# Spreading the small products of a triangular inverse over four tiles of TensorE, and moving one product into their first visit

## The chip, the cores and the metric

The kernel runs on one core of a Trainium2 chip. The metric is the device time of one execution in microseconds (us); lower is better. Before the change it is 2568.02 us, the median of three runs (2565.74 to 2568.44).

## What is computed

One layer of a streaming encoder, for 1024 new frames and 32 frames of a running stream. Every frame goes through a normalisation, one large combined projection, and then two groups of heads: differential attention, and an RWKV-7 recurrence whose state is a 64x64 matrix per head. The two results are gated, joined and projected back, and the input is added. Cut to what matters here:

```python
xn = rms_norm(x, norm_g)
proj = xn @ w_in                      # q, k, v, g_att, p_rw, g_rw
o  = diff_attention(q, keys, vals, q_pos, k_pos, lam)
...
def step(S, inp):                     # one token of the recurrence
    r_t, w_t, k_t, v_t, a_t, b_t = inp
    sa = jnp.einsum('bhij,bhj->bhi', S, a_t)
    S = S * w_t[:, :, None, :] + sa[..., None] * b_t[:, :, None, :] + v_t[..., None] * k_t[:, :, None, :]
    y = jnp.einsum('bhij,bhj->bhi', S, r_t)
    return S, y
...
out = jnp.concatenate([att_out, rw_out], axis=-1) @ w_out
return x + out, k, v, s_final, p_rw[:, -1:]
```

## The kernel before, in words

**Projections.** The tokens are worked on in two halves, A (544 columns, in pieces of 288 and 256) and B (512 columns). `proj` (L102 is the line of the matmul helper `mm` that it calls) multiplies one 128-column block of weights by all tokens: 16 steps of k, three products each (a high and a low part of weights and of tokens), into a PSUM tile `pj`. The weights come as raw pieces `wr` by DMAs issued on GpSimd's queue (POOL, L241), ScalarE rounds them to `wh` (ACT, L234), VectorE forms the rest `wl` (DVE, L235).

**Streams.** All other work is cut into generators (`chs`, `dns`, `qks`, `ats` and so on) that are called between the matmuls of a projection. `clk` is a running estimate of TensorE's time that `mm` adds to (with a divisor `ways`) and `shaped` adds 95 ns to whenever the tile shape of a product changes; a generator yields a delay from the table `LAT`, and its next part is issued at the first call at which `clk` has passed that delay. The chain stream `chs` is called after every step of k, the others after two or four. TensorE executes everything in the order in which it was issued, so that a product that comes before its operand is ready holds all the projections behind it.

**The recurrence.** It is done by chunks of 64 tokens. For each pair of heads (u, 16 in all with both halves) there are two sub-blocks of four chunks, except that in half A the second has five: 32 sub-blocks, 24 with cn = 4 and 8 with cn = 5, each with ng = 2 cn blocks (a chunk and one of two heads). A token's update inside a chunk needs the inverse of a unit triangular 64x64 matrix. Its two 32x32 diagonal blocks are inverted on VectorE (the loop of L799 and L801 in `rw_down`), go to DRAM (`dt`) and come back; the block that joins them is the product of three 32x32 matrices.

**The chain of a sub-block, `rw_chain`.** It first transposes V into the upper 64 rows of `UV` (L844 and L845 read it out of PSUM), loads the inverses into `TT` (the matrix that is put together) and into `t01` (a tile with tag k2, which the trace calls `k`), and has VectorE transpose a part of them (L861). Then come three visits to TensorE, with a yield between each two, in which other work is issued. All three write the one PSUM tile `ch`:

1. ng products 32x32, of the strict block of `MM` with `u0`, into rows 32 to 63 of `ch`; ScalarE reads them out as `wt` (L866), into rows 32 to 63 of `UV`.
2. after `t10`, ng products 32x32, of `wt` with `t01`, into rows 0 to 31; ScalarE reads them into `TT` in two pieces (L873).
3. after `x0`, ng products 64x64, of the strict part of `MM` with V; ScalarE reads them back into `MM` in two pieces (L880).

A product of float32 stands in the trace as two weight loads and two matmuls, so that a visit of ng = 8 has 16 matmuls and one of ng = 10 has 20. Every product of the first visit uses the same 32x32 tile of the array, as does every one of the second; those of the third lie in rows 64 to 127 of the array and go by turns to columns 0 to 63 and 64 to 127. After the three visits the chain walks over its chunks one by one (three products each, delays `c0` to `c3`); L931 is VectorE's last read of `ch` for a chunk.

Of the kernel before, what the change touches and what calls it, by code (L numbers as in the profile page):

```python
# [46 lines left out]
def build(tc, I, O):  # L47
    nc = tc.nc
    V, S, G, PE = nc.vector, nc.scalar, nc.gpsimd, nc.tensor
# [6 lines left out]
    def T(shape, tag, dt=F32, bufs=1):  # L56
        cnt[0] += 1
        return sb.tile(shape, dt, tag=tag, name=f"{tag}_{cnt[0]}", bufs=bufs)

    def PT(tag, bufs, shape=(128, 512)):  # L60
        cnt[0] += 1
        return ps.tile(list(shape), F32, tag=tag, name=f"{tag}_{cnt[0]}", bufs=bufs)
# [6 lines left out]
    def bank(tag, shape=(128, 512)):  # L69
        if tag not in held:  # L70
            held[tag] = PT(tag, 1, shape)
        return held[tag]
# [14 lines left out]
    def shaped(k, m):  # L87
        now = tuple(next(z for z in (32, 64, 128) if x <= z) for x in (k, m))
        if now != mode[0]:
            clk[0] += 95.0  # L90
            mode[0] = now

    def mm(out, lhsT, rhs, start=True, stop=True, ways=1):
        n, m = 1, 1
        for d in rhs.shape[1:]:
            n *= d
        for d in lhsT.shape[1:]:
            m *= d
        shaped(lhsT.shape[0], m)
        load = 0.83 * m + 5.0  # L100
        clk[0] += (max(0.4375 * n + 6.0, load) if rhs.dtype == F32R else 2 * max(0.84 * n, load)) / ways
        PE.matmul(out, lhsT, rhs, start=start, stop=stop)  # L102

    def tr(out, in_, idn):
        shaped(*in_.shape)
        clk[0] += 110.0
        PE.transpose(out, in_, idn)  # L107
# [73 lines left out]
    def dma(out, in_):  # L181
        if out.dtype == F32R:
            out, in_ = out.bitcast(F32), in_.bitcast(F32)
        nc.sync.dma_start(out, in_)
# [83 lines left out]
    for k, tag in enumerate(RAW):  # L268
# [7 lines left out]
        a, eng = (acc[1], G) if pool else (acc[0], V)  # L276
# [141 lines left out]
    def lat(key, half):  # L418
        return LAT[key + "AB"[half]]
# [262 lines left out]
    def flat(t):  # L682
        return t.rearrange("p c t -> p (c t)")
# [43 lines left out]
    def after(sub, stream, kind, back):  # L727
        j = sub - back
        return lambda: j < 0 or (kind, j // 2, j % 2) in stream.done
# [98 lines left out]
    def rw_chain(half, i, sub, st):  # L828
        lo, hi = SUBS[half][sub]
        cn = hi - lo  # L830
        ng = 2 * cn
        gsub = 2 * (8 * half + i) + sub
        AR, MM, MMg, dt, t_m = (st[sub][n] for n in ("AR", "MM", "MMg", "dt", "t_m"))
        PL, v = st["PL"], st["v"]
        UV = T([128, cn, 2, 64], "UV")
        UVf = UV.rearrange("p c h t -> p c (h t)")
        yield lat("bk0", half)
        p = bank("ch")
        for j in range(2):
            tr(p[:, 128 * j:128 * j + 128], flat(v)[:, 64 * lo + 128 * j:64 * lo + 128 * j + 128], ident)  # L840
        if cn == 5:
            tr(p[0:64, 256:384], v[:, 8, :], ident)
        pv = p[:, 0:256].rearrange("p (a b) -> p a b", b=128)
        S.copy(UVf[64:128, 0:4:2, :], pv[0:64])  # L844
        S.copy(UVf[64:128, 1:4:2, :], pv[64:128])  # L845
        if cn == 5:
            S.copy(UVf[64:128, 4, :], p[0:64, 256:384])
        if sub == 1:
            chs.done.add(("vread", 8 * half + i))
        TT = TTb[:, 0:cn]  # L850
        dtg = dt.rearrange("b (c h) s t -> b h s c t", h=2)
        for b in range(2):
            for h in range(2):
                o = 64 * h + 32 * b
                dma(TT[o:o + 32, :, o:o + 32], dtg[b, h, 0:32])
        t01 = T([64, ng, 32], "k2")
        for b in range(2):
            dma(t01[32 * b:32 * b + 32], dt[b, :, 0:32, :].rearrange("g s t -> s g t"))
        UVg = UVf.rearrange("p c t -> p (c t)")[0:64, 0:32 * ng].rearrange("p (g t) -> p g t", t=32)
        u0, wt = UVg[0:32], UVg[32:64]  # L860
        V.transpose(u0.rearrange("p g t -> p (g t)"), t01[0:32].rearrange("p g t -> p (g t)"))  # L861
        yield max(1500, t_m + lat("tt", half) - clk[0])
        p = bank("ch")
        for g in range(ng):
            mm(p[32:64, 32 * g:32 * g + 32], MMg[0:32, g, 32:64], u0[:, g, :])
        S.copy(wt, p[32:64, :32 * ng].rearrange("p (a b) -> p a b", b=32))  # L866
        yield lat("t10", half)
        p = bank("ch")
        for g in range(ng):
            mm(p[0:32, 32 * g:32 * g + 32], wt[:, g, :], t01[32:64, g, :])  # L870
        pg = p[0:32, :32 * ng].rearrange("p (c h b) -> p c h b", h=2, b=32)
        for h in range(2):
            S.copy(TT[64 * h:64 * h + 32, :, 64 * h + 32:64 * h + 64], pg[:, :, h, :])  # L873
        yield lat("x0", half)
        p = bank("ch")
        for c in range(cn):
            for h in range(2):
                mm(p[64 * h:64 * h + 64, 64 * c:64 * c + 64], MM[64:128, c, h, 0:64], UV[64:128, c, h, :])
        for h in range(2):
            S.copy(MM[0:64, :, h, 0:64], p[64 * h:64 * h + 64, :64 * cn].rearrange("p (c v) -> p c v", v=64))  # L880

        yield after(gsub, pos, "post", 1)
        Y = T([128, 3, 128], "Yt")
        if sub == 0:
            Sw = T([128, 2, 64], "Sw")
            G.memset(Sw, 0.0)
            if half == 1:
                for h in range(2):
                    dma(Sw[64 * h:64 * h + 64, h, :], Spast[i, 64 * h:64 * h + 64, :])
            st["Sw"] = Sw  # L890
        order = [4, 0, 1, 2, 3] if cn == 5 else [0, 1, 2, 3]
        key = "c0"
        for c in order:
            gc = lo + c
            if c == 4:
                S_ = T([128, 2, 64], "S0")
                G.memset(S_, 0.0)
                for h in range(2):
                    dma(S_[64 * h:64 * h + 64, h, :], I["S0"][i, 64 * h:64 * h + 64, :])
            else:  # L900
                S_ = st["Sw"]
            Sf = S_.rearrange("p h t -> p (h t)")
            yield lat(key, half)
            key = "c1"
            ch = bank("ch")
            mm(ch[:, 0:128], AR[:, c].rearrange("p a t -> p (a t)"), Sf)
            RS = T([128, 128], "RS")
            S.copy(RS[high], ch[high, 0:128])  # L908
            xs = T([128, 64], "xs")
            for h in range(2):  # L910
                V.tensor_tensor(xs[64 * h:64 * h + 64], ch[low, 64 * h:64 * h + 64], MM[low, c, h, 0:64], op=ALU.add)  # L911
            SP = T([64, 2, 64], "SP")
            for h, hr in enumerate((low, high)):
                S.activation(SP[:, h, :], S_[hr, h, :], AF.Copy, scale=PL[hr, 0, gc:gc + 1])  # L914
            yield lat("c2", half)
            mm(ch[:, 128:192], TT[:, c, :], xs)
            S.copy(UV[low, c, 0, :], ch[low, 128:192])
            V.tensor_copy(UV[low, c, 1, :], ch[high, 128:192])  # L918
            yield lat("c3", half)
            for h in range(2):  # L920
                mm(ch[:, 192 + 64 * h:256 + 64 * h], MM[:, c, h, 64:192], UV[:, c, h, :])
            for h, hr in enumerate((low, high)):
                V.scalar_tensor_tensor(S_[hr, h, :], ch[low, 192 + 64 * h:256 + 64 * h], PL[low, h, gc:gc + 1],  # L923
                                       SP[:, h, :], ALU.mult, ALU.add)
            if c == 4:
                V.tensor_tensor(Y[0:64, 2, :], ch[high, 192:320], RS[high], op=ALU.add)
                G.memset(Y[64:128, 2, :], 0.0)
                for h in range(2):
                    dma(O["wkvs"][i, 64 * h:64 * h + 64, :], S_[64 * h:64 * h + 64, h, :])
            else:  # L930
                V.tensor_tensor(Y[64 * (c % 2):64 * (c % 2) + 64, c // 2, :], ch[high, 192:320], RS[high],  # L931
                                op=ALU.add)
                if gc == 7:
                    for h in range(2):
                        dma((Spast, O["wkvp"])[half][i, 64 * h:64 * h + 64, :], S_[64 * h:64 * h + 64, h, :])
        st[sub]["Y"] = Y
# [64 lines left out]
    for u in range(16):  # L1001
        half, i = divmod(u, 8)
        n, ncnk, chunks = (NA, NB)[half], (9, 8)[half], CHUNKS[half]
# [171 lines left out]
```

## Time and profile before

| what | before |
|---|---|
| median of three runs | 2568.02 us |
| lowest, highest | 2565.74, 2568.44 us |
| the profiled execution | 2568.85 us |
| its span, first to last instruction | 2567.1 us |
| mean granted TensorE clock | 0.993 of full speed |
| instructions | 48812 |
| TensorE matmul busy | 2482.5 us (97%) |
| VectorE, ScalarE, GpSimd busy | 1884.4 (73%), 1366.2 (53%), 414.1 us (16%) |

The span is what the rows of the trace add up to; 1.75 us of the profiled execution lie around it. In rows of the trace PE is TensorE's matmuls, PEld its weight loads, DVE VectorE, ACT ScalarE, POOL GpSimd and SP the queue that issues most DMAs. A matmul's duration counts from its first column to the end of a modelled pipeline, so that matmuls overlap: what one costs is the step from its start to the next one's start.

### The profile page before, as it was taken

The numbers are of one execution on the slowest core, as the hardware profiler recorded it, in microseconds if no ns is written. First come the engines' busy times: TensorE is split into PE (matmuls) and PEld (weight loads), VectorE is DVE, ScalarE is ACT, GpSimd is POOL, SyncE is SP. The second block draws the span as 40 slices with busy tenths as digits, with TensorE's granted clock in tenths as the row PEclk, the third lists the DMA queues.
The fourth block names the chain that finished last, engine by engine and source line by source line (L and its number), as shares of the span: only waits on it lengthen the run. The fifth ranks groups of instructions, "written<-read, shape, count | busy, mean of one in ns | idle before, by whom it ended". The sixth has DMA issues, their size and how long they took to land.

```text
span 2567.1 us, 48812 instructions
## 1 busy us (share of the span) xinstructions
PE 2482.5 (97%) x17128; PEld 2189.9 (85%) x17128; DVE 1884.4 (73%) x5704; ACT 1366.2 (53%) x3210; POOL 414.1 (16%) x949
## 2 busy tenths in 40 slices
PE   7999999999999999999999999999999999999999
PEld 7999999899998899977777777877777778999887
DVE  6577777777777787788788888887878888653432
ACT  6455555555556555565555555656565556232321
POOL 3211111111111111111111111111111111111000
PEclk8999999999999999999999999999999999999999
DMA  5333333333344424343333333333333345545443
GB/s 163 111 103 107 101 97 96 103 93 108 90 118 133 121 75 123 104 141 98 96 102 93 105 94 105 94 105 94 105 91 104 89 128 149 148 139 151 144 140 106
DMA packets 198662, 286.71 MB, mean 112 GB/s; under 512 B 102096, under 2 KB 115920, under 8 KB 198416
## 3 DMA queue, kind: packets, MB, share of 16 engines
q0 software_dynamic: 51088, 169.12, 22.2%
q1 hardware_dynamic: 147328, 114.47, 15.8%
q8 instruction: 135, 2.21, 0.4%
q14 instruction: 111, 0.91, 0.1%
HBM read 228.11 MB, written 37.51 MB: 103 GB/s over the span
## 4 chain that ended last, share of the span: by engine, by line
PE 64%; DVE 20%; DMA 5%; ACT 5%; issue 4%; SPq 1%; POOL 0%; DVEq 0%; ACTq 0%; POOLq 0%
PE pj L102 48%; PE ch L102 6%; DVE wl L235 4%; PE am L102 3%; DVE ts L801 3%; DVE tm L799 3%; PE sc L102 2%; PE Y L102 2%; ACT wh L234 1%; DVE Sw L923 1%; PE sc L107 1%; PE am L107 1%; DVE ca L715 1%; DMA E<-x_prompt 1%; DMA wr<-w_in 1%
## 5 line engine op out<-in xcount | busy, mean ns | idle before, releaser
L102 PE MATMUL pj<-xh,wh 128*128 128x256 f32 (+2 forms) x3888 | 1314.4, 338 | 11.8 <-ACT xh L258 6.7
L102 PE MATMUL pj<-xl,wh 128*128 128x256 f32 (+2 forms) x3888 | 1267.1, 326 | 4.1 <-DVE xl L259 4.0
L102 PE MATMUL pj<-xh,wl 128*128 128x256 f32 (+2 forms) x3888 | 1265.9, 326 | 1.1 <-DVE wl L235 1.1
L102 PEld LDWEIGHTS pj<-xh,wh 128*128 128x128 f32 x3888 | 738.4, 190 | 64.7 <-ACT xh L258 6.7
L102 PEld LDWEIGHTS pj<-xh,wl 128*128 128x128 f32 x3888 | 738.1, 190 | 55.5 <-DVE wl L235 2.6
L102 PEld LDWEIGHTS pj<-xl,wh 128*128 128x128 f32 x3888 | 739.4, 190 | 47.7 <-DVE xl L259 6.1
L234 ACT CAST wh<-wr 128x512 fp32r<-128x512 f32 x584 | 360.6, 618 | 412.8 <-PE pj L102 361.8
L235 DVE TENSOR_TENSOR wl<-wr,wh 128x512 fp32r<-128x512 f32 x584 | 401.1, 687 | 175.8 <-ACT wh L234 168.2
L241 POOL DMA_DIRECT2D wr<-w_in x517 | 277.8, 537 | 1549.2 <-DVE wl L235 653.0
L801 DVE TENSOR_TENSOR ts<-tm,ts 64x54 f32<-64x54 f32 (+35 forms) x992 | 197.9, 200 | 15.7
L799 DVE TENSOR_TENSOR tm<-ts,ms 64x54 f32<-64x54 f32 (+35 forms) x992 | 197.8, 199 | 14.9
L102 PEld LDWEIGHTS ch<-UV,MM 64*64 64x64 f32 (+2 forms) x1632 | 112.6, 145 | 41.4 <-DVE UV L918 15.5
L914 ACT ACTIVATE SP<-Sw,PL 64x64 f32<-64x64 f32 x256 | 88.4, 345 | 103.4 <-DVE Sw L923 86.0
L102 PE MATMUL ch<-UV,MM 64*64 64x64 f32 (+2 forms) x1632 | 126.2, 230 | 8.3 <-DVE UV L918 5.4
L235 DVE TENSOR_TENSOR wl<-MM,wh 128x512 fp32r<-128x512 f32 x64 | 44.0, 689 | 89.2 <-ACT wh L234 89.2
L234 ACT CAST wh<-MM 128x512 fp32r<-128x512 f32 x64 | 39.6, 620 | 128.9 <-PE pj L102 123.0
L923 DVE SCALAR_TENSOR_TENSOR Sw<-ch,PL,SP 64x64 f32<-64x64 f32 x256 | 70.6, 276 | 33.0 <-PE ch L102 25.1
L911 DVE TENSOR_TENSOR xs<-ch,MM 64x64 f32<-64x64 f32 x272 | 58.6, 216 | 39.0 <-ACT RS L908 33.2
L102 PE MATMUL am<-Vt,E 128*128 128x128 f32 (+1 forms) x592 | 79.8, 277 | 2.3 <-DVE asg L526 2.3
L102 PEld LDWEIGHTS am<-Vt,E 128*128 128x128 f32 (+1 forms) x592 | 72.4, 189 | 7.5 <-DVE asg L526 2.7
L102 PE MATMUL sc<-Ks,Qd 128*128 128x512 f32 (+2 forms) x224 | 74.6, 345 | 1.5 <-ACT E L610 1.3
L610 ACT ACTIVATE E<-sc,sm 128x640 f32<-128x640 f32 (+3 forms) x64 | 61.0, 953 | 26.9 <-DVE sm L609 24.3
(305 smaller groups left out, 3149.9 us busy)
## 6 DMA issues: line engine op xcount, KB each, us to landing
wr<-w_in POOLq DMA_DIRECT2D x517, 256.0 KB, 3.3
wr<-w_out POOLq DMA_DIRECT2D x64, 256.0 KB, 3.6
MM<-w_out POOLq DMA_DIRECT2D x32, 512.0 KB, 4.0
t<-xB SPq DMA_DIRECT2D x32, 256.0 KB
ms<-dm SPq DMA_DIRECT2D x96, 64.0 KB
t<-t SPq DMA_DIRECT2D x64, 68.0 KB
t<-mixd SPq DMA_DIRECT2D x16, 272.0 KB
t<-xA SPq DMA_DIRECT2D x16, 272.0 KB
```

Source lines behind the costliest of these rows:

```text
L102: PE.matmul(out, lhsT, rhs, start=start, stop=stop)
L107: PE.transpose(out, in_, idn)
L234: S.copy(wh, raw)
L235: V.tensor_tensor(wl, raw, wh.bitcast(F32), op=ALU.subtract)
L241: q.dma_start(raw, wsrc[:, g * 512:(g + 1) * 512].rearrange("p (k f) -> p k f", k=4))
L610: S.activation(E[c][:, :nk], sc[:, :nk], AF.Exp, bias=mx[:, c:c + 1], scale=SCALE, accum_out=l[:, c:c + 1])
L715: V.tensor_tensor_scan(c_[:, c], ones[:, 0:64], c_[:, c], 0.0, ALU.mult, ALU.add)
L799: V.tensor_tensor(tm, ts_[:, 0:qn, s:s + 1].to_broadcast([R * nb, qn, m]), ms[:, s:s + 1, s + 1:32].to_broadcast([R * nb, qn, m]), op=ALU. ...
L801: V.tensor_tensor(ts_[:, 0:qn, s + 1:32], tm, ts_[:, 0:qn, s + 1:32], op=ALU.add)
L911: V.tensor_tensor(xs[64 * h:64 * h + 64], ch[low, 64 * h:64 * h + 64], MM[low, c, h, 0:64], op=ALU.add)
L914: S.activation(SP[:, h, :], S_[hr, h, :], AF.Copy, scale=PL[hr, 0, gc:gc + 1])
L923: V.scalar_tensor_tensor(S_[hr, h, :], ch[low, 192 + 64 * h:256 + 64 * h], PL[low, h, gc:gc + 1], SP[:, h, :], ALU.mult, ALU.add)
```

## The change

The strict 32x32 blocks are copied by GpSimd (four copies for each sub-block) into a tile `mq` of 128 rows, and the inverses are loaded into `t0` and `t1` in the same layout: block g = 4j + q lies in rows 32q to 32q + 31. With that, the products of q = 0 to 3 lie on the four diagonal 32x32 tiles of the array and write four different quarters of the partitions of `ch`. VectorE's transpose and ScalarE's reading of the first product now take 128 rows at once (with five chunks a second piece of 64 rows); the second product is read into `TT` in four pieces in place of two. With five chunks each load takes two DMAs. The 64x64 products with V move from a visit of their own to the first one, behind the 32x32 products, and one yield falls away. The products' estimates are divided by 4 and 2 in `clk`; the table `LAT` is left as it was.

```diff
--- before.py
+++ after.py
@@ -853,31 +853,44 @@
             for h in range(2):
                 o = 64 * h + 32 * b
                 dma(TT[o:o + 32, :, o:o + 32], dtg[b, h, 0:32])
-        t01 = T([64, ng, 32], "k2")
-        for b in range(2):
-            dma(t01[32 * b:32 * b + 32], dt[b, :, 0:32, :].rearrange("g s t -> s g t"))
-        UVg = UVf.rearrange("p c t -> p (c t)")[0:64, 0:32 * ng].rearrange("p (g t) -> p g t", t=32)
-        u0, wt = UVg[0:32], UVg[32:64]
-        V.transpose(u0.rearrange("p g t -> p (g t)"), t01[0:32].rearrange("p g t -> p (g t)"))
+        J = (cn + 1) // 2
+        t0, t1, mq, u0 = (T([128, 3, 32], tag) for tag in ("t0q", "t1q", "mq", "u0q"))
+        for b, tq in enumerate((t0, t1)):
+            dma(tq[:, 0:2, :], dt[b, 0:8, 0:32, :].rearrange("(j q) s t -> (q s) j t", q=4))
+            if cn == 5:
+                dma(tq[0:64, 2, :], dt[b, 8:10, 0:32, :].rearrange("q s t -> (q s) t"))
+        quads = [(q, slice(32 * q, 32 * q + 32), (cn - q // 2 + 1) // 2) for q in range(4)]
+        for q, r, n in quads:
+            G.tensor_copy(mq[r, 0:n, :], MM[0:32, q // 2:cn:2, q % 2, 32:64])
+
+        def whole(f, out, in_):
+            f(out[:, 0:2, :].rearrange("p j t -> p (j t)"), in_[:, 0:64])
+            if cn == 5:
+                f(out[0:64, 2, :], in_[0:64, 64:96])
+
+        whole(V.transpose, u0, t0.rearrange("p j t -> p (j t)"))
         yield max(1500, t_m + lat("tt", half) - clk[0])
         p = bank("ch")
-        for g in range(ng):
-            mm(p[32:64, 32 * g:32 * g + 32], MMg[0:32, g, 32:64], u0[:, g, :])
-        S.copy(wt, p[32:64, :32 * ng].rearrange("p (a b) -> p a b", b=32))
-        yield lat("t10", half)
-        p = bank("ch")
-        for g in range(ng):
-            mm(p[0:32, 32 * g:32 * g + 32], wt[:, g, :], t01[32:64, g, :])
-        pg = p[0:32, :32 * ng].rearrange("p (c h b) -> p c h b", h=2, b=32)
-        for h in range(2):
-            S.copy(TT[64 * h:64 * h + 32, :, 64 * h + 32:64 * h + 64], pg[:, :, h, :])
-        yield lat("x0", half)
-        p = bank("ch")
+        for j in range(J):
+            for q, r, n in quads:
+                if j < n:
+                    mm(p[r, 320 + 32 * j:352 + 32 * j], mq[r, j, :], u0[r, j, :], ways=4)
         for c in range(cn):
             for h in range(2):
-                mm(p[64 * h:64 * h + 64, 64 * c:64 * c + 64], MM[64:128, c, h, 0:64], UV[64:128, c, h, :])
+                mm(p[64 * h:64 * h + 64, 64 * c:64 * c + 64], MM[64:128, c, h, 0:64], UV[64:128, c, h, :], ways=2)
+        wt = T([128, 3, 32], "t0q")
+        whole(S.copy, wt, p[:, 320:416])
         for h in range(2):
             S.copy(MM[0:64, :, h, 0:64], p[64 * h:64 * h + 64, :64 * cn].rearrange("p (c v) -> p c v", v=64))
+        yield lat("t10", half)
+        for j in range(J):
+            for q, r, n in quads:
+                if j < n:
+                    mm(p[r, 416 + 32 * j:448 + 32 * j], wt[r, j, :], t1[r, j, :], ways=4)
+        for q, r, n in quads:
+            h = q % 2
+            S.copy(TT[64 * h:64 * h + 32, q // 2:cn:2, 64 * h + 32:64 * h + 64],
+                   p[r, 416:416 + 32 * n].rearrange("p (j b) -> p j b", b=32))
 
         yield after(gsub, pos, "post", 1)
         Y = T([128, 3, 128], "Yt")
```

## Rows read from the trace of the kernel before

**Rows 1.** The page: span, and busy time of each engine.

```profile
span 2567.1 us, 48812 instructions
PE 2482.5 (97%) x17128; PEld 2189.9 (85%) x17128; DVE 1884.4 (73%) x5704; ACT 1366.2 (53%) x3210; POOL 414.1 (16%) x949
```

**Rows 2.** The page: the chain that ended last, by engine.

```profile
PE 64%; DVE 20%; DMA 5%; ACT 5%; issue 4%; SPq 1%; POOL 0%; DVEq 0%; ACTq 0%; POOLq 0%
```

**Rows 3.** Groups by form on PE: xcount | busy us, mean ns | idle before.

```profile
L102 PE MATMUL ch<-k,UV 32*32 32x32 f32 x544 | 23.5, 194 | 6.5 <-ACT UV L866 6.5
L102 PE MATMUL ch<-UV,MM 64*64 64x64 f32 x544 | 23.3, 227 | 0.8 <-ACT TT L873 0.8
```

**Rows 4.** PE's timeline at a first visit, ng = 8: start us, us.

```profile
1173.20 0.39 PE L102 MATMUL pj<-xl,wh 128*128 128x512 f32 x1
1173.43 0.40 PE L102 MATMUL pj<-xh,wl 128*128 128x512 f32 x1
1173.76 0.69 PE L102 MATMUL ch<-UV,MM 32*32 32x32 f32 x16
1174.37 0.50 PE L102 MATMUL pj<-xh,wh 128*128 128x512 f32 x1
1174.72 0.39 PE L102 MATMUL pj<-xl,wh 128*128 128x512 f32 x1
```

**Rows 5.** PE's timeline: a second visit with 64-row products right behind it.

```profile
601.33 0.69 PE L102 MATMUL ch<-k,UV 32*32 32x32 f32 x16 [0.45 <-ACT UV L866]
601.95 0.37 PE L102 MATMUL Y<-AR,BK 64*128 64x128 f32 x1
601.96 0.37 PE L102 MATMUL am<-AR,BK 64*128 64x128 f32 x1
```

**Rows 6.** PE's timeline at the third visit of the sub-block of rows 4.

```profile
1179.56 0.40 PE L102 MATMUL pj<-xh,wl 128*128 128x512 f32 x1
1179.89 0.68 PE L102 MATMUL ch<-UV,MM 64*64 64x64 f32 x16
1180.50 0.50 PE L102 MATMUL pj<-xh,wh 128*128 128x512 f32 x1
1180.84 0.39 PE L102 MATMUL pj<-xl,wh 128*128 128x512 f32 x1
```

**Rows 7.** PE's timeline: a first visit with ng = 10.

```profile
394.80 0.81 PE L102 MATMUL ch<-UV,MM 32*32 32x32 f32 x20
```

**Rows 8.** Timeline: a chain product behind VectorE's last read of the tile.

```profile
862.02 0.29 DVE L931 TENSOR_TENSOR Yt<-ch,RS 64x128 f32<-64x128 f32 x1
...
862.37 0.49 PE L102 MATMUL ch<-Sw,AR 128*128 128x128 f32 x2 [0.48 <-DVE Yt L931]
```

**Rows 9.** ScalarE's reads of `ch`, by line: ns min/median/max, first and last start.

```profile
L866 ACT COPY UV<-ch x32: 362/363/418, 213.6 to 2283.1; 32x256 f32<-32x256 f32 x24, 32x320 f32<-32x320 f32 x8
L873 ACT COPY TT<-ch x64: 238/254/282, 216.0 to 2285.7; 32x128 f32<-32x128 f32 x48, 32x160 f32<-32x160 f32 x16
L880 ACT COPY MM<-ch x64: 349/368/425, 217.5 to 2287.8; 64x256 f32<-64x256 f32 x48, 64x320 f32<-64x320 f32 x16
```

**Rows 10.** Waits of PEld: waited for, us in total, times, longest.

```profile
PEld ch L102 <- ACT UV L866: 8.0, 7, 3.3
...
PEld ch L102 <- ACT TT L873: 4.1, 11, 1.0
```

**Rows 11.** Groups by form on POOL and ACT: xcount | busy us, mean ns | idle before.

```profile
L241 POOL DMA_DIRECT2D wr<-w_in x517 | 277.8, 537 | 1549.2 <-DVE wl L235 653.0 <-DVE tm L799 278.3 <-DVE ts L801 261.4
...
L478 POOL COPY kb<-t 128x32 f32<-128x32 f32 x8 | 3.2, 399 | 4.4 <-DVE t L450 4.2
...
L234 ACT CAST wh<-wr 128x512 fp32r<-128x512 f32 x584 | 360.6, 618 | 412.8 <-PE pj L102 361.8 <-DMA wr<-w_in 25.6 <-DMA wr<-w_out 17.6
```

**Rows 12.** The loads of `t01` on the SP queue, and VectorE's transpose.

```profile
L184 SPq DMA_DIRECT2D k<-dt x64: 336/448/1239, 201.5 to 2263.8; - x64
L861 DVE STREAM_TRANSPOSE UV<-k x32: 422/432/500, 205.1 to 2269.5; 32x256 f32<-32x256 f32 x24, 32x320 f32<-32x320 f32 x8
```

## The prediction

> **What bounds the kernel.** I read the page's busy times first: TensorE's matmuls are busy 2482.5 of 2567.1 us [rows 1], which leaves 84.6 us of idle time. Then the chain that ended last: TensorE has 64% of it, VectorE 20% [rows 2]. So time taken off TensorE's in-order queue should come off the span nearly one for one, unless the other engines, which the chain also passes through, turn it into waiting. The groups by form say how often the products in question occur: 544 matmuls in the second visit, 544 in the third, and by the code as many in the first [rows 3]. Their busy times of 23 us each count overlapping pipelines and are not their cost; the cost is read from the timeline, from the last projection matmul before a visit to the second one after it.
>
> **What a visit costs now.** At a first visit with 16 matmuls it is 1173.43 to 1174.72, 1.29 us, where two plain steps would take 2 x 0.23: the visit costs 0.83 us [rows 4]. A second visit has the same 0.69 us from first start to last end [rows 5], so 0.83 again. The third takes 1179.56 to 1180.84, 1.28 us, and costs 0.82 [rows 6]. Inside a first visit the starts spread over 0.69 - 0.19 = 0.50 us [rows 3, 4], 0.033 us from one matmul to the next; the other 0.33 us is the way in and out: the array changes its tile shape twice, and the first matmuls of either side come late. With 20 matmuls the group lasts 0.81 instead of 0.69 us [rows 7]: 0.12 more, so 0.95; for a third visit I add the four matmuls at its mean spacing, (0.68 - 0.23) / 16 = 0.028 us, 0.12 with rounding [rows 3, 6], so 0.94. A sub-block costs 2.48 us with four chunks and 2.84 with five.
>
> **Step 1, four tiles.** Now all 32x32 products of a visit queue for one tile. The trace of before has no four tiles at once, so I bound the new spacing. From above: 0.033 us, no gain. From below: four products in the time of one. Nearest are the two-tile rows. Matmuls of 64x64, twice as wide, follow each other by 0.028 us on two tiles, less than the 0.033 of the narrow ones on one [rows 4, 6], and two products on different rows of the array start 0.01 us apart [rows 5]. Both say that different tiles work side by side and that a start itself costs under 0.01 us; four of those fit into 0.033. So I take the lower bound: 16 matmuls go in 4 rounds, 3 x 0.033 + 0.03 for staggered starts = 0.13 us in place of 0.50. With five chunks there are 6 rounds (the last block row has two products only), 0.20 in place of 0.62. A second visit then costs 0.83 - 0.37 = 0.46 us, or 0.95 - 0.42 = 0.53.
>
> The Trainium skill speaks against this: its page "TensorE: Matmul & The Clock Gate", section "Wait — 56ns, not 53.3ns?", says that starts of matmuls never come closer than about 25 ns however few columns they have. By it 16 matmuls would need 0.40 us, an estimate, and the sum below would be some 13 us instead of 31. The two starts 0.01 us apart [rows 5] do not agree with it across tiles, and I go by the row.
>
> **Step 2, one visit less.** The third visit's products now follow the 32x32 ones. The new first visit is the old third, 0.82 us, plus the narrow part, 0.13, plus one change of shape inside: from the last 32x32 start (601.33 + 0.69 - 0.19 = 601.83) to the next product of 64 rows at 601.95 it is 0.12 us [rows 3, 5]. Together 1.07 us; with five chunks 0.94 + 0.20 + 0.12 = 1.26.
>
> Per sub-block: 1.07 + 0.46 = 1.53 against 2.48, 0.95 us less, 24 times 22.8 us; with five chunks 1.26 + 0.53 = 1.79 against 2.84, 1.05 less, 8 times 8.4 us. Sum: **31.2 us** off TensorE's queue.
>
> **Step 3, ScalarE's reads.** A chain product waits for the last read of the whole tile `ch`, whatever the columns: the product at 862.37 stood 0.48 us until L931 ended at 862.31, and by the code it neither reads what L931 makes nor writes the columns L931 reads [rows 8]. Now the second visit waits for L866 alone, 0.36 us. After the change the two reads of L880, 0.37 us each, come behind the read of `wt` in the same queue and touch the same tile, so that it waits for some 0.7 us more [rows 9]. The delay `t10` of 1.0 us, in which projections are issued, covers most of it. Weight loads stood for L866 7 times, 8.0 us in all [rows 10]; if each of these grows by 0.7, it is 5 us. The ends are 0 and 32 x 0.7 = 22. In return the third visit's wait for L873, 4.1 us [rows 10], goes. I take +1 us for both. What is late next is the read into `TT`: four pieces, at most 0.25 us each (their like of twice the width) [rows 9], 1.0 us where it was 0.5. The first chain product behind it has a delay of 1.3 us or more: zero; without that cover 32 x 0.5 = 16.
>
> **Edits costed at nothing.** GpSimd gets 128 copies, at most 0.40 us each (the row has four times the partitions) [rows 11]: 1.6 us per sub-block, between weight loads on the same queue. GpSimd idles 1549 us in front of those loads [rows 11], which hides it; if not, up to 51 us. The copies wait for `MM`, written long before by the code, and for last round's products; the first visit that needs them comes only after the solve. SP gets 16 more loads of 0.45 us [rows 12] on a queue that the whole span covers; 7 us otherwise. VectorE's transpose (0.43 us [rows 12]) sees a quarter of the columns, and nothing on TensorE waits for it. ScalarE has two more short reads per sub-block, under 0.5 us, at 53% busy [rows 1].
>
> **Step 4, the order.** The planner charges each sub-block about 1.3 us less (by the code: 0.50 becomes 0.13 twice, 0.93 becomes 0.46, two shape changes go), so everything behind is issued at other points, and the 84.6 us of idle [rows 1] are dealt anew. No row says which way. The delays in `LAT` stay those of the old order; I take 5% worse, +4 us, and let it run from -6 to +12.
>
> **Sum.** -31.2 + 1 + 4 = -26 us. Against the profiled execution's 2568.85 that is 2542.7; the median of the runs stands 0.8 below that execution, so I forecast **2542 us**, 1.0% less. About 0.2%, 5 us, is what a measurement of this kernel can tell from no change.
>
> **Rivals.**
> (a) The four tiles take turns. No row has tiles of different rows write one PSUM bank: the pair at 601.95 goes to two tiles `Y` and `am` [rows 5], the pairs of the third visit share their rows. Then the narrow part stays 0.50 and 0.62 us; a sub-block costs 0.82 + 0.50 + 0.12 + 0.83 = 2.27, or 2.63, 0.21 less in either case, 6.7 us, and with +5 the time is 2566. Chance 0.12. The Trainium skill, "TensorEngine Tiling (Array Packing)", section "Gotcha 1: PSUM Pressure", says that different row tiles cannot use one PSUM bank at once, which is what this rival would need the hardware to enforce; the trace has no case of it.
> (b) Only two go side by side, as every pair of rows does: 8 rounds, 0.26 us, or 10, 0.33. The first visit costs 0.82 + 0.26 + 0.12 = 1.20, the second 0.59; with five chunks 1.39 and 0.66. That is 0.69 x 24 + 0.79 x 8 = 22.9 us, 18 after the other terms: 2550. Chance 0.12.
> (c) TensorE gains the 31 us but hands a part back as waiting, since it has only 64% of the chain [rows 2]: 0.64 x 31 = 20, less 5, 2553. Against it speaks the 97% [rows 1]. Chance 0.08.
> (d) Slower: GpSimd's copies make weight loads late. A load for the next group sits behind four copies, up to 1.6 us; if all of it reaches TensorE at each of 32 chains it is 51 us, and the time 2568 - 26 + 51 = 2593. It decides from 0.8 us per chain on. For it: only two buffers `wr`. Against it: ScalarE's 584 casts waited for landings 25.6 + 17.6 us and for TensorE 361.8 [rows 11], so weights mostly lie ready. Chance 0.04.
> Anything else 0.02; the forecast case has 0.62.
>
> **Range and chances.** The forecast case with its unknown costs at their good ends is 2568 - 31 - 6 = 2531, with a second visit that always waits (22) and the order at +4 it is 2568 - 31 + 22 + 4 = 2563. 2531 to 2564 holds nearly all of it, (b) and (c), and a part of (a). Faster by over 0.2% are the forecast case, (b), (c) and a third of (a): 0.84. Within 0.2%: half of (a) and edges, 0.09. Slower: 0.07.
>
> **What would show it.** Second visits of 16 matmuls that last 0.13 + 0.19 = 0.32 us instead of 0.69 prove step 1; 0.45 would be (b), 0.69 (a). Only 64 visits in place of 96, with 64x64 products 0.12 us behind the 32x32, prove step 2. Second visits waiting for ScalarE's reads of the first by over 15 us in all would prove step 3 too low; casts waiting for `wr` well over 43 us would be (d). TensorE's idle time far from 85 us would show step 4 mis-sized. The forecast is wrong if the visits shrink as said and the span does not.

## The result, and the profile after

The changed kernel takes 2522.55 us (median of four runs, 2518.54 to 2524.22) against 2568.22 us for the kernel before (also four runs, one more than the three on which the forecast rests); the ratio is 0.9822, with an interval of 0.9805 to 0.9839. That is 46 us less, where 26 were forecast, and the time lies under the stated range of 2531 to 2564. On another chip the same program later gave 2525.62 us and 0.9848 (0.983 to 0.9866), 39 us less. The profiled execution has 2521.34 us.

The first lines of the page after the change, answering to [rows 1]:

```profile
span 2519.6 us, 49104 instructions
PE 2448.6 (97%) x17128; PEld 2160.8 (86%) x17128; DVE 1870.8 (74%) x5712; ACT 1365.4 (54%) x3282; POOL 458.4 (18%) x1077
```

Here is the reading that the rest of this text hangs on. The span is TensorE's busy time plus its idle time. Busy time fell from 2482.5 to 2448.6, by 33.9 us; idle, the span less that, fell from 84.6 to 71.0, by 13.6 us. The forecast had the first number at 31.2 and the second at 5 us the other way.

The timeline of TensorE at a first visit of 16 and 16 matmuls, then at a second visit, after the change (start us, us); they answer to [rows 4] and [rows 6]:

```profile
211.11 0.28 PE L102 MATMUL pj<-xl,wh 128*128 128x256 f32 x1
211.23 0.28 PE L102 MATMUL pj<-xh,wl 128*128 128x256 f32 x1
211.43 0.33 PE L102 MATMUL ch<-u0q,mq 32*32 32x32 f32 x16
211.69 0.68 PE L102 MATMUL ch<-UV,MM 64*64 64x64 f32 x16
212.30 0.39 PE L102 MATMUL pj<-xh,wh 128*128 128x256 f32 x1
212.52 0.28 PE L102 MATMUL pj<-xl,wh 128*128 128x256 f32 x1
...
1161.10 0.39 PE L102 MATMUL pj<-xl,wh 128*128 128x512 f32 x1
1161.32 0.40 PE L102 MATMUL pj<-xh,wl 128*128 128x512 f32 x1
1161.65 0.33 PE L102 MATMUL ch<-t1q,t0q 32*32 32x32 f32 x16
1161.91 0.50 PE L102 MATMUL pj<-xh,wh 128*128 128x512 f32 x1
1162.24 0.40 PE L102 MATMUL pj<-xl,wh 128*128 128x512 f32 x1
```

A narrow group lasts 0.33 us where it lasted 0.69. Less the 0.19 us of one matmul, 16 starts take 0.14 us; 0.13 was forecast. The first visit takes 211.23 to 212.52, 1.29 us, less two plain steps of 0.12: 1.05 (forecast 1.07). The second takes 1161.32 to 1162.24, 0.92, less 2 x 0.22 to 0.23: 0.46 to 0.48 (forecast 0.46). Between the last narrow start (211.43 + 0.33 - 0.19 = 211.57) and the first wide one lies 0.12 us, as forecast.

ScalarE's reads by line after the change (ns min/median/max, first and last start), and the weight loads that waited for them, answering to [rows 9] and [rows 10]. L867 is the read of `wt`, L884 that of the products with V, L892 that into `TT`:

```profile
L867 ACT COPY t0q<-ch x32: 194/210/215, 214.7 to 2229.1; 128x64 f32<-128x64 f32 x32
...
L884 ACT COPY MM<-ch x64: 349/369/429, 214.8 to 2229.6; 64x256 f32<-64x256 f32 x48, 64x320 f32<-64x320 f32 x16
...
L892 ACT COPY TT<-ch x128: 185/205/231, 216.0 to 2231.8; 32x64 f32<-32x64 f32 x112, 32x96 f32<-32x96 f32 x16
```

```profile
PEld ch L102 <- ACT MM L884: 5.5, 14, 0.8
...
PEld ch L102 <- ACT TT L892: 1.5, 5, 0.6
```

The second visit now waits for L884, the reads behind the one that it needs, as the forecast said: weight loads waited 5.5 us for it, in 14 waits, where they had waited 8.0 us for L866. The matmuls themselves stood 1.8 us of it.

Groups of GpSimd and ScalarE, answering to [rows 11] (xcount | busy us, mean ns | idle before):

```profile
L241 POOL DMA_DIRECT2D wr<-w_in x517 | 277.8, 537 | 1440.8 <-DVE wl L235 565.1 <-DVE ts L801 302.5 <-DVE tm L799 302.4
...
L864 POOL COPY mq<-MM 32x64 f32<-32x64 f32 x112 | 31.8, 284 | 39.7 <-DVE MM L780 28.6 <-PE ch L102 5.8
...
L234 ACT CAST wh<-wr 128x512 fp32r<-128x512 f32 x584 | 360.9, 618 | 469.5 <-PE pj L102 388.2 <-DMA wr<-w_in 54.3 <-DMA wr<-w_out 7.2
```

The copies take 0.28 us each. ScalarE's casts waited 54.3 + 7.2 = 61.5 us for weights to land, 18 more than before.

### The profile page after: what moved, and what is told of

Its sections match the earlier page's. It is cut to its first block, busy times and chain, and to the rows that moved or that the text cites. A ratio compares the mean times of both kernels' runs of the same rounds, so it can differ in the third digit from the quotient of the medians.

```text
span 2519.6 us, 49104 instructions
## 1 busy us (share of the span) xinstructions
PE 2448.6 (97%) x17128; PEld 2160.8 (86%) x17128; DVE 1870.8 (74%) x5712; ACT 1365.4 (54%) x3282; POOL 458.4 (18%) x1077
## 4 chain that ended last, share of the span: by engine, by line
PE 48%; DVE 9%; ACT 3%; issue 3%; DMA 2%; POOL 0%; SPq 0%; DVEq 0%; ACTq 0%; POOLq 0%
PE pj L102 37%; PE ch L102 4%; PE am L102 2%; PE sc L102 2%; DVE wl L235 2%; DMA wr<-w_in 1%; DVE tm L799 1%; DVE ts L801 1%; PE Y L102 1%; PE sc L107 1%; ACT wh L234 1%; PE am L107 1%; DVE MM L780 0%; DVE Sw L936 0%; PE Y L107 0%
## 5 line engine op out<-in xcount | busy, mean ns | idle before, releaser
L102 PEld LDWEIGHTS ch<-UV,MM 128*128 128x128 f32 (+1 forms) x1088 | 92.8, 162 | 15.9 <-DVE UV L931 9.0
L102 PE MATMUL ch<-UV,MM 128*128 128x64 f32 (+1 forms) x1088 | 102.5, 246 | 2.2 <-DVE UV L931 1.8
L936 DVE SCALAR_TENSOR_TENSOR Sw<-ch,PL,SP 64x64 f32<-64x64 f32 x256 | 70.4, 275 | 31.0 <-PE ch L102 25.7
```

## Experiments

Three theories were put against each other for the 13.6 us of idle time. **Planner:** the lower charges in `clk` give an order with less waiting. **Structure:** a chain with one visit less waits less. **Deal:** any change of the order in which work is issued deals the waits anew, as cards are dealt, with no direction, and this pair happened to be a good one. The experiments ran in groups, each beside the kernel before on the same chip; the ratios below are to that.

**E1, the change's products, the charges of before**

```diff
-                    mm(p[r, ...], mq[r, j, :], u0[r, j, :], ways=4)
+                    mm(p[r, ...], mq[r, j, :], u0[r, j, :])
...
+        clk[0] += 95.0
         wt = T([128, 3, 32], "t0q")
```

(and in the same way without `ways` in the other two products)

> The changed kernel, but the planner charges every sub-block what it charged before (no division by 4 and 2, and 95 ns more for the visit that fell away). The products are those of the change: the narrow groups last 0.13 + 0.19 us. If the lower charges gave the order with less idle time (the planner theory), TensorE's idle time goes back from 71 to about 85 us and the time to about 2536. If the idle time fell because the chain has one visit and its waits less (the structure theory), idle stays near 71 and the time near 2523. If the order is merely dealt anew with no direction (the deal theory), idle lies anywhere from 65 to 90, 2517 to 2542.

Measured 2527.18 us, ratio 0.9859 (0.9844 to 0.9873). Page:

```profile
span 2528.1 us, 49088 instructions
PE 2446.2 (97%) x17128; PEld 2161.3 (85%) x17128; DVE 1867.7 (74%) x5712; ACT 1372.5 (54%) x3282; POOL 467.2 (18%) x1077
```

Idle time is 81.9 us, nearest to the 85 of the planner theory, though its 2536 was not reached; both values also lie in the wide spans of the deal theory.

**E2, the products of before, the charges of the change**

```diff
-            mm(p[32:64, ...], MMg[0:32, g, 32:64], u0[:, g, :])
+            mm(p[32:64, ...], MMg[0:32, g, 32:64], u0[:, g, :], ways=4)
```

(`ways=4` and `ways=2` in the other two visits, and 95 ns taken off `clk` in the third)

> The kernel before, its products untouched, but the planner charges what it charges after the change. Planner theory: idle falls from 85 to about 71 us, 2554. Structure theory: idle stays at 85, 2568. Deal theory: anything from 2560 to 2580.

Measured 2558.45 us, 0.9976 (0.9965 to 0.9988), just outside the deal theory's span. Page:

```profile
span 2553.3 us, 48823 instructions
PE 2478.1 (97%) x17128; PEld 2182.0 (85%) x17128; DVE 1882.5 (74%) x5704; ACT 1366.2 (54%) x3210; POOL 417.9 (16%) x949
```

Idle time is 75.2 us, again nearer to the planner theory's 71 than to the structure theory's 85. The products are those of before, and the time differs by 0.24%.

**E3, only the four tiles**: the 64x64 products and their read stand in a third visit again, behind `yield lat("x0", half)`.

> Only the four tiles: the products with V keep a third visit of their own behind a yield, as before. By the sum of the forecast the visits lose 2 x 0.37 us (24 times) and 2 x 0.42 us (8 times), 24.5 us: 2543 with the idle time of before. Structure theory: the idle time stays near that of before, as three visits stay, so 2543. Planner theory: idle falls by some 14 us here too, 2530.

Measured 2549.68 us, 0.9945 (0.993 to 0.996). Page:

```profile
span 2547.9 us, 49102 instructions
PE 2459.9 (97%) x17128; PEld 2160.7 (85%) x17128; DVE 1877.9 (74%) x5712; ACT 1370.1 (54%) x3282; POOL 451.8 (18%) x1077
```

Busy time fell by 22.6 us, about the 24.5 that the sum gives. Idle time is 88.0, near the structure theory's 85 and against the planner theory, which wanted some 70; the time missed the values of both, 2543 and 2530.

**E4, only the merge, in sub-blocks of four chunks**

```diff
+        if cn == 4:
+            for c in range(cn):
+                for h in range(2):
+                    mm(p[64 * h:64 * h + 64, 64 * c:64 * c + 64], MM[64:128, c, h, 0:64], UV[64:128, c, h, :])
```

(behind the first visit's products, which move to columns 256 and up of `ch`; the read follows that of `wt`, and the third visit stays for five chunks)

> Only the merge, and only in the 24 sub-blocks of four chunks: all 32x32 products on one tile as before, the products with V behind them in the first visit, charges as before. By the sum of the forecast 24 x 0.21 = 5 us less: 2563. Structure theory: 24 of 32 third visits with their waits are gone, so most of the 14 us of idle time goes too, about 2553. Planner theory: 2563.

Measured 2549.63 us, 0.9946 (0.993 to 0.9963), near structure's 2553. Page, and the wait of the second visit's weight loads (L874 is the read of the products with V here):

```profile
span 2547.5 us, 48833 instructions
PE 2470.6 (97%) x17128; PEld 2184.0 (86%) x17128; DVE 1886.9 (74%) x5704; ACT 1365.0 (54%) x3210; POOL 416.3 (16%) x949
```

```profile
PEld ch L102 <- ACT MM L874: 9.2, 17, 0.8
```

Idle time is 76.9; busy time fell by 11.9 us where 5 were expected, so busy time too moves by some us for another reason, probably the granted clock (see below). The wait for the reads behind `wt` shows here as well, 9.2 us in 17 waits.

**E5 to E12, eight other orders.** No product, tile or wait is touched; only a number in the planner's charges is changed, so that all other work is issued at other points:

```diff
-            clk[0] += 95.0
+            clk[0] += 80.0
```

E5 and E6 are the kernel before with 80 and 110, E7 and E8 the changed kernel with 80 and 110. E9 to E12 leave that and replace 0.4375 ns per column of a projection matmul by 0.42 and 0.455: E9 and E10 in the kernel before, E11 and E12 in the changed one.

> The kernel before with its products and layout untouched; the planner charges 80 instead of 95 ns for a change of tile shape, so that all other work is issued at other points. Deal theory (idle time and slow-clock time are dealt anew by any change of order): the time moves by up to 12 us either way, 2556 to 2580, with idle time between 72 and 97 us. Structure theory: only the chain's own visits matter, the time stays within 3 us of 2565.

> The same with 110 instead of 95 ns, an order that differs from that of before in more places. Deal theory: 2556 to 2580, not the same value as the run with 80 ns. Structure theory: within 3 us of 2565. Planner theory (lower charges give less idle): slower than the run with 80 ns, by some 5 us.

> The changed kernel with 80 instead of 95 ns charged for a change of shape. Deal theory: 2522 was a good deal, so the time is likelier above it: 2520 to 2540, idle 70 to 95 us. Structure theory: within 3 us of 2522, idle near 71 us.

> The changed kernel with 110 instead of 95 ns. Deal theory: 2520 to 2540, another value than the run with 80 ns. Structure theory: within 3 us of 2522, idle near 71 us.

> The kernel before, products untouched; the planner charges 0.42 instead of 0.4375 ns per column of a projection matmul, which moves most issue points. So far four orders of the old products had 2478 to 2486 us of TensorE busy and 70 to 85 us idle, four orders of the new ones 2446 to 2449 busy and 68 to 82 idle. Deal theory: busy 2478 to 2486 again, idle anywhere from 68 to 90, time 2548 to 2575. Structure theory (the change itself lowers the idle time by ten or more): idle over 80.

> The kernel before with 0.455 in place of 0.4375. Deal theory: busy 2478 to 2486, idle 68 to 90, 2548 to 2575. Structure theory: idle over 80.

> The changed kernel with 0.42. Deal theory: busy 2445 to 2450, idle 68 to 90, 2515 to 2540. Structure theory: idle under 75, 2515 to 2525.

> The changed kernel with 0.455. Deal theory: busy 2445 to 2450, idle 68 to 90, 2515 to 2540. Structure theory: idle under 75, 2515 to 2525.

Medians, ratios to the kernel before with their intervals, and from the pages the mean granted clock (1 is full speed), TensorE's busy time and the span less that (us). A page is of one execution: that of E6 took 2558.21 us, 8 us more than the median.

| products | order | median | ratio | clock | busy | idle |
|---|---|---|---|---|---|---|
| old | before | 2568.22 | 1 | 0.993 | 2482.5 | 84.6 |
| old | E2 | 2558.45 | 0.9976 (0.9965 to 0.9988) | 0.996 | 2478.1 | 75.2 |
| old | E5 | 2562.13 | 0.9987 (0.9977 to 0.9997) | 0.994 | 2482.4 | 80.6 |
| old | E6 | 2550.12 | 0.9941 (0.9924 to 0.9957) | 0.993 | 2485.7 | 70.4 |
| old | E9 | 2553.61 | 0.996 (0.9947 to 0.9973) | 0.997 | 2473.3 | 72.9 |
| old | E10 | 2555.36 | 0.997 (0.9958 to 0.9981) | 0.994 | 2481.5 | 70.5 |
| new | after | 2522.55 | 0.9822 (0.9805 to 0.9839) | 0.997 | 2448.6 | 71.0 |
| new | E1 | 2527.18 | 0.9859 (0.9844 to 0.9873) | 0.996 | 2446.2 | 81.9 |
| new | E7 | 2521.87 | 0.9834 (0.9814 to 0.9854) | 0.996 | 2446.2 | 76.1 |
| new | E8 | 2517.62 | 0.9816 (0.9801 to 0.9831) | 0.996 | 2448.1 | 68.0 |
| new | E11 | 2538.61 | 0.9905 (0.989 to 0.9919) | 0.994 | 2456.5 | 82.5 |
| new | E12 | 2538.17 | 0.9905 (0.9891 to 0.992) | 0.995 | 2450.7 | 90.0 |

Two of the twelve pages, E6 and E12, the old products with least and the new ones with most idle time:

```profile
span 2556.1 us, 48851 instructions
PE 2485.7 (97%) x17128; PEld 2192.1 (86%) x17128; DVE 1874.0 (73%) x5704; ACT 1364.9 (53%) x3210; POOL 438.9 (17%) x949
```

```profile
span 2540.7 us, 49115 instructions
PE 2450.7 (96%) x17128; PEld 2162.2 (85%) x17128; DVE 1867.5 (74%) x5712; ACT 1369.3 (54%) x3282; POOL 460.6 (18%) x1077
```

The two columns on the right decide it. Busy time separates the kernels in every order: 2473 to 2486 against 2446 to 2457, means 2480.6 and 2449.4, a difference of **31.2 us**, the forecast's sum. By the scatter of the orders this difference is good to some 5 us, an estimate, so the agreement to the tenth is luck. Idle time does not separate them: 70 to 85 against 68 to 90, means 75.7 and 78.3. A page repeats more closely than that: E15 below, the changed kernel once more, has 73.0 us of idle time where the first page has 71.0.

Structure falls: E11 and E12 should have stayed under 75 us of idle time, E9 and E10 over 80, and E6 within 3 us of 2565. Planner falls too: E6, with the higher charges, should have been some 5 us slower than E5; it was 12 us faster, with 70.4 us of idle time against 80.6. Deal remains, but it had named its spans too narrow: E2, E6 and E8 were 2 to 6 us faster than they allow, and the busy times of E9 and E11, 2473.3 and 2456.5, lie some 5 and 7 us outside.

Those two busy times go with the granted clock: E9 has the highest of the old products, E11 the lowest of the new ones. Work at the lower level of the clock takes up to nearly twice as long (0.24 against 0.13 us for a projection step, last section). So by the mean clocks, 0.9945 and 0.9957, up to some 3 of the 31.2 us are the clock's and not the products'; in the recorded pair, with 0.993 and 0.997, up to some 10 of the 33.9. Both are estimates.

The kernel before is the slowest of six orders of its products and the recorded change one of the better of its own: that pair flatters the change. By the mean ratios, 0.9972 and 0.9857, it is worth 1.15%, 30 us, which the scatter of twelve orders leaves uncertain by some 10 us (an estimate).

**E13, tile by tile**

```diff
-        for j in range(J):
-            for q, r, n in quads:
-                if j < n:
-                    mm(p[r, ...], mq[r, j, :], u0[r, j, :], ways=4)
+        for q, r, n in quads:
+            for j in range(n):
+                mm(p[r, ...], mq[r, j, :], u0[r, j, :], ways=4)
```

(and so in the second visit)

> The changed kernel with the 32x32 products of a visit issued tile by tile (both or all three of tile 0, then tile 1 and so on) in place of tile 0, 1, 2, 3, 0, 1 and so on; all other work keeps its place. If a product can pass those in front of it on another tile, nothing changes: groups of 16 start within 0.14 us and the time stays at 2522. If the starts keep their order, so that tile 1 waits until tile 0 has its last, 16 starts take about 13 x 0.032 = 0.41 us; each visit costs some 0.28 us more (0.35 with 20), 19 us in all, 2541, with the idle time of the changed kernel, since its order is kept: a price of the four tiles inside one deal.

Measured 2528.61 us, 0.9867 (0.984 to 0.9894), against 0.9848 of the changed kernel's second measurement: not to be told apart; the interval of its first one, 0.9805 to 0.9839, ends just below. The timeline of TensorE, second visits of 16 and of 20 matmuls here:

```profile
218.20 0.35 PE L102 MATMUL ch<-t1q,t0q 32*32 32x32 f32 x16 [1.04 <-ACT MM L883]
...
256.11 0.50 PE L102 MATMUL ch<-t1q,t0q 32*32 32x32 f32 x20
```

and the second visit of 20 in the changed kernel:

```profile
253.30 0.38 PE L102 MATMUL ch<-t1q,t0q 32*32 32x32 f32 x20
```

Neither expectation holds. Two products for a tile behind each other cost 0.02 us per visit (0.35 against 0.33), far from the 0.28 of starts that keep their order; three cost 0.12 us (0.50 against 0.38). Nearly all other visits of the two traces last as long as those shown. It looks as if TensorE passes over a product that waits for its tile, but not over any number of them; that is an inference, and only these two cases were tried. In all it is 48 x 0.02 + 16 x 0.12 = 2.9 us, too little to tell by the busy time: 2452.2, against 2448.6 and, in E15, 2451.7 of the changed kernel.

**E14, GpSimd's copies three times**

```diff
+            for _ in range(3):
-            G.tensor_copy(mq[r, 0:n, :], MM[0:32, q // 2:cn:2, q % 2, 32:64])
+                G.tensor_copy(mq[r, 0:n, :], MM[0:32, q // 2:cn:2, q % 2, 32:64])
```

> The changed kernel with each of GpSimd's copies made three times, 256 more of 0.28 us, 2.3 us more per sub-block on the queue of the weight loads. If the copies delay weight loads (the rival of the forecast that ends slower), casts wait for landings longer than the 61 us of the changed kernel and the time rises by 10 us or more. If they lie in GpSimd's idle time, the time stays within 4 us of 2522.

Measured 2531.93 us, 0.9874 (0.9854 to 0.9895), clear of the changed kernel's first interval (0.9805 to 0.9839), and overlapping the second (0.983 to 0.9866) at its edge. Page, and the casts' group:

```profile
span 2529.7 us, 49360 instructions
PE 2447.8 (97%) x17128; PEld 2160.0 (85%) x17128; DVE 1875.6 (74%) x5712; ACT 1365.5 (54%) x3282; POOL 533.3 (21%) x1333
...
L234 ACT CAST wh<-wr 128x512 fp32r<-128x512 f32 x584 | 361.0, 618 | 475.1 <-PE pj L102 389.8 <-DMA wr<-w_in 58.4 <-DMA wr<-w_out 9.9
```

With the order kept, busy time stays and idle time rises from 71.0 (73.0 in E15) to 81.9. The 256 copies cost 6 to 9 us by the two medians of the changed kernel and 7 to 13 by its two ratios, near the 10 that the rival's expectation named. By which wait they do so stays open. Casts wait 68.3 us for landings, but with single copies it is 70.4 in E13 (60.1 + 10.3), and with none 72.8 in E6 (62.5 + 10.3): this wait follows the order, not the copies.

**E15 to E17, without GpSimd's copies.** E15 is the changed kernel again. E16 lets the SP queue bring the blocks, and E17 does so with 110 in place of 95 ns, the order of E8:

```diff
-            G.tensor_copy(mq[r, 0:n, :], MM[0:32, q // 2:cn:2, q % 2, 32:64])
+            dma(mq[r, 0:n, :], MM[0:32, q // 2:cn:2, q % 2, 32:64])
```

> The changed kernel as it is, on the chip of the next two, to compare them with. 2519 to 2525, idle 71 us.

> The changed kernel with the blocks brought into place by four DMAs from the SP queue, in place of GpSimd's four copies. Three times the copies cost some 10 us, so by proportion the 128 copies cost 5 us: then 2517, and casts wait less than 61 us for landings. If the copies cost nothing and only the third threefold copy found no idle place, 2522.

> The same with 110 ns charged for a change of shape, the order that gave 2518 with GpSimd's copies: 2513 if the copies cost 5 us there too, 2518 if not; the deal of the order may move it by 6 either way.

E15 took 2525.62 us, 0.9848; E16 2522.23, 0.9837 (0.9821 to 0.9852), idle 68.6; E17 **2513.0**, 0.9802 (0.9785 to 0.9818), idle 64.3, against 0.9816 for E8. Both are lower than with the copies, by 3.4 and 4.6 us, but the intervals overlap, so this alone is inconclusive. Casts wait 58.5 us for landings in E16, against 63.8 in E15. E17 has the lowest time of all runs here. Its page:

```profile
span 2512.4 us, 49147 instructions
PE 2448.1 (97%) x17128; PEld 2163.4 (86%) x17128; DVE 1869.4 (74%) x5712; ACT 1363.2 (54%) x3282; POOL 426.4 (17%) x949
```

## Why the prediction was wrong, step by step

- **What bounds the kernel: right.** Busy time taken off TensorE came off the span. Rival (c), a part handed back as waiting, is not seen: mean idle time is 75.7 and 78.3 us, 2.6 apart, with a spread of 14 and 22 us inside the groups.
- **Step 1, four tiles: right.** 0.14 us for 16 starts where 0.13 was forecast, 0.38 - 0.19 = 0.19 for 20 where it was 0.20. Rivals (a) and (b) are out. The rule of the Trainium skill's page "TensorE: Matmul & The Clock Gate", section "Wait — 56ns, not 53.3ns?", that starts keep 25 ns apart does not agree with the trace across tiles: 16 in 0.14 us. Nor did the four tiles take turns for writing one PSUM bank, which by the Trainium skill's page "TensorEngine Tiling (Array Packing)", section "Gotcha 1: PSUM Pressure", tiles of different rows cannot access at once: here they wrote different quarters of its partitions, and went side by side, 16 starts in 0.14 us.
- **Step 2, one visit less: right.** 1.05 us for the new first visit, 0.12 for the change of shape inside it. The visits so bear out the terms of the sum of 31.2 us. Busy time agrees with it within its scatter of some 5 us: 31.2 us between the means of six orders each, some 28 if the clock's share is taken off.
- **Step 3, the reads: right in kind, and in size only over several orders.** In the recorded pair the two waits fell, from 8.0 + 4.1 to 5.5 + 1.5 us, where +1 was forecast; 3.3 of the 8.0 us were one read behind a late cast (last section). In the mean of the six orders of each kernel, weight loads waited 4.7 us for the read before a second visit with the old products (L866) and 8.7 us with the new ones (L884); these 4 us more are within the 5 that the forecast allowed. For the reads into `TT` they waited 3.9 and 3.6 us, so that wait did not go but moved to the next product.
- **Edits costed at nothing: probably off by a few us.** GpSimd's copies last 0.28 us, under the 0.40 of the bound, but 256 more cost 6 to 13 us (E14); in proportion the change's 128 cost 3 to 7, an estimate, and E16 and E17 point the same way without proving it. Rival (d) is out in its size, 51 us. Its sign did show, casts that wait 61.5 us for landings in place of 43.2, but the old products have 72.8 in E6: the order does that without any copy.
- **Step 4, the order: this is the step that failed.** It was put at "5% worse, +4 us", to "run from -6 to +12". In the recorded pair idle time fell by 13.6 us, where steps 3 and 4 together had it rise by 5. The mean over orders, +2.6 us, is near that +5; what was mis-sized is the spread. Idle time is 70 to 85 us in six orders of the same old products and 68 to 90 in six of the new ones, so the difference of an old and a new deal runs from -17 to +20. The forecast also had no term for the clock, which by the estimate above took up to some 10 us off the busy time in this pair. And it took the profiled order of before as a middle one, and it is the worst of six: it started from 84.6 us, where the mean is 75.7. No row of one trace says this; it takes other orders of the same work.

## What to carry to other kernels

Where a program issues its order by estimates, a change of the program is two changes, one of cost and one of order; take the first from the visits and from busy time at like granted clocks, and give the second a range from a few runs in which nothing but a charge of the planner is altered. A comparison of one order with one order measured this change at 46 us, of which some 30 are its own by the mean over six orders each. Small products that fill a quarter of the array's rows and columns are worth laying out on the diagonal: here four went in the time of one (16 starts in 0.14 us in place of 0.50), and most of what then remains of a visit is the change of shape, so visits should be joined.

## What the runs showed of the hardware

A stall can cost more than its length. In the kernel before, TensorE stood from about 2230.0 us for the read of a visit whose queue, ScalarE's, held a late weight cast. The windows around it (us, PE, PEld, DVE, ACT and POOL busy, granted clock, DMA share, GB/s) and the timeline:

```profile
2229.00:2233.00 4.00, 1.00 (x8) 0.77 (x6) 0.36 (x1) 0.98 (x2) 0.00 (x0) 0.86 0.68 201
2233.00:2243.00 10.00, 9.96 (x69) 9.50 (x70) 5.84 (x27) 1.86 (x5) 0.54 (x1) 0.54 0.08 28
2243.00:2253.00 10.00, 10.00 (x82) 10.00 (x82) 9.07 (x39) 3.50 (x9) 1.83 (x4) 1.00 0.42 127
```

```profile
2229.57 0.30 PE L102 MATMUL pj<-xl,wh 128*128 128x288 f32 x1
2229.71 0.29 PE L102 MATMUL pj<-xh,wl 128*128 128x288 f32 x1
2231.99 0.62 ACT L234 CAST wh<-wr 128x512 fp32r<-128x512 f32 x1 [4.67 <-DMA wr<-w_out]
2232.63 0.36 ACT L866 COPY UV<-ch 32x256 f32<-32x256 f32 x1
...
2233.05 1.06 PE L102 MATMUL ch<-k,UV 32*32 32x32 f32 x16 [3.04 <-ACT UV L866]
...
2234.68 0.44 PE L102 MATMUL pj<-xh,wl 128*128 128x288 f32 x1
2234.92 0.44 PE L102 MATMUL pj<-xh,wh 128*128 128x288 f32 x1
```

After 3.0 us of idle time the granted clock is 0.54 for ten microseconds, mostly the lower of the two levels, 1.2 GHz in place of 2.4: a projection step takes 0.24 us instead of 0.13 to 0.14, a visit of 16 lasts 1.06 instead of 0.69. This shows as busy time, so a deal can move busy time too. The clock also differs between executions of one order: the four of E6 took 2548.32, 2549.27, 2550.97 and 2558.21 us at mean granted clocks of 0.998, 0.997, 0.996 and 0.993. So the clock belongs beside every busy time that is compared; what sets it from one execution to the next was not tried.
